# Three moves of single instructions in an RWKV time-mixing kernel: two products, five small copies, one scaling

## The chip, the core and the metric

The kernel runs on one core of a Trainium2 chip. The metric is the device time of one execution in microseconds. Before the change the median of 12 runs is 202.87 us, the lowest 202.19, the highest 204.02.

Five engines take part, each working through its own instructions in the order in which they were written: TensorE (PE, matmuls and transposes), VectorE (DVE), ScalarE (ACT), GpSimd (POOL) and SyncE (SP, which here issues DMAs). An instruction that needs a result of another engine waits on a semaphore, and all that stands behind it on its engine waits with it.

## The reference, cut to what matters

```python
x_prev[:, 1:, :] = x[:, :-1, :]                     # the row before, zero for the first
xv = x * time_mix_v + x_prev * (1 - time_mix_v)
xr = x * time_mix_r + x_prev * (1 - time_mix_r)
v = xv @ value_weight
r = xr @ receptance_weight
out = (sigmoid(r) * v) @ output_weight
```

x is 16 x 2048 x 256, float32. The key product k is computed by the reference but not used in its output, and the kernel leaves it away.

## The kernel before, in words

The 16 batches of 2048 rows are cut into 64 units of 512 rows (`NU`), four to a batch. The data is held transposed, channels on the 128 partitions, in two halves of the 256 channels (`ko` 0 and 1), as bf16. A unit u goes through these steps:

- Its rows are transposed into a tile `xt`, by PE and a copy on ACT (L207, L223), or, for the last five batches, by a transposing DMA on SP (L188). A batch's `xt` has one slot more than the batch has row groups: slot 0 holds the last group shifted by one column, so that the "row before" is the slot before. For batches 2 to 10 DVE makes this shifted slot (L427). For batches 11 to 15, whose rows come by DMA, ACT makes it (L550), in the windows 41, 45, 49, 53 and 57.
- Its two mixes, R and V, are formed in a tile `mix`. The mix of a row is c times the row before, plus the row, and a factor goes into the weights. First come the **products** `mix = xt * c`: the half ko = 0 mostly on DVE (L257, `scale`), the half ko = 1 of many early V mixes, and of all mixes from unit 10 on, on POOL (L267, `scale_pool`); from unit 10 on a product is for two units together (128x1024). Of the late units' V mixes the half ko = 0 is made on ACT (L514, `scale_act`). Then comes the **add** `mix = mix + xt` on DVE (L279, `add`).
- PE multiplies mix R by the receptance weights into `psum_r` (four matmuls, L287), ACT takes the sigmoid into `s_sb` (L535). PE multiplies mix V by the value weights into `psum_v` (L287), DVE forms z = s * psum_v (L580).
- PE multiplies z by the output weights into `psum_o` (eight matmuls, L311), ACT copies that to `o_sb` (L345), SP stores it.

`psum_r`, `psum_v` and `psum_o` have one buffer each. So the value matmuls of a unit wait until z of the unit before has been read out of `psum_v`, the receptance matmuls until the sigmoid before has read `psum_r`, and the output matmuls until the copy before has read `psum_o`.

The order is written out by hand: one pass of the loop at L522, a **window** g, issues for all engines what is to be done while unit g is projected. In the text r8, v8, z8, s8 and o8 are the receptance matmuls, value matmuls, z, sigmoid and output (matmuls, or the copy of them) of unit 8; "8R" and "8V" are its mixes. In a window PE does r_g, transposes for later units, v_g and o_(g-1); from unit 39 on (`LATE_O`) r_g, o_(g-2), v_g and no more transposes. DVE does the products due in this window, adds, z_g, and then the adds that are `held` until behind z. POOL does the products of `pooled[g]`, each made to wait for the last add in front of z_g (`scale_pool(p, last)`, L588). ACT does s_g, the copies of transposed rows, the copy of an output, and its products.

Lists built at L482 to L509 say which product and add is due in which window. In window 6 (`AHEAD`) DVE has, in front of z6: three products of unit 7 (7R both halves, 7V one half), two products of unit 8 (8R both halves, 128x512 each), the adds of 7R and 7V. The add of 8R is held behind z6. Mix V of the units 40 and 41 has its product for ko = 0 on ACT in window 38, since `FREE` is 38 and the test at L554 is `g >= FREE`. In the windows 41, 45, 49, 53 and 57 ACT does the sigmoid, then the shifted slot (L550), then the output's copy (L345). The product of POOL in these windows (mix R of units 44, 48, 52, 56, 60, the first of their batches) reads slot 0 of the new `xt`, so it needs this shifted slot as well as the last add.

Of the kernel before, what the change touches and what calls it, by code (L numbers as in the profile page):

```python
# [15 lines left out]
def kernel(  # L16
# [25 lines left out]
    nc = tc.nc  # L42

    B, S, D = x.shape
    P = 128
    KO = D // P
    J = S // P
    UJ = 4
    TU = UJ * P
    UB = J // UJ  # L50
# [4 lines left out]
    H = UJ // 2  # L55
    BYDMA = 5 * UB
    CROSS = NU - BYDMA - LOOK
    FREE = CROSS
    LATE_O = CROSS
    WAITING = {33: 38, 35: 39, 37: 43, 39: 43, 45: 51, 47: 51}  # L60
    START_T = [1, 3, 5, 6, 7, 9, 11, 12]
    AHEAD = 6
# [21 lines left out]
    xt = {}  # L84
# [14 lines left out]
    def unit_rows(t, b, e, n=1):  # L99

        return t[b, e * TU : (e + n) * TU, :].rearrange("(e p j) d -> p e j d", p=P, j=UJ)
# [21 lines left out]
    for m, tm in enumerate([time_mix_r, time_mix_v]):  # L123
        nc.scalar.dma_start(
            out=tm_rows[m * KO : (m + 1) * KO, :], in_=tm.rearrange("(ko p) -> ko p", p=P)
        )
    for h in (1, 0):
        nc.sync.dma_start(
            out=x_unit[:, 0, h * H : (h + 1) * H], in_=unit_rows(x, 0, 0)[:, 0, h * H : (h + 1) * H, :]
        )  # L130
    nc.sync.dma_start(
        out=w_f32[:, 0], in_=receptance_weight.rearrange("(ko p) n -> p ko n", p=P)
# [110 lines left out]
    def slots(piece, off=0):  # L243

        b, _, lo, hi = piece
        j = lo // P + (lo // TU if b < BYUNIT else 0) + off
        return slice(j, j + (hi - lo) // P)

    def mixed(piece):
        b, m, lo, hi = piece  # L250
        j = lo // P % (2 * UJ)
        return mix[(b * S + lo) // (2 * TU)][:, m, j : j + (hi - lo) // P]

    def scale(piece, kos=(0, 1)):
        b, m, _, _ = piece
        for ko in kos:
            nc.vector.tensor_scalar(  # L257
                out=mixed(piece)[:, :, ko],
                in0=xt[b][:, slots(piece), ko],
                scalar1=c_sb[:, m, ko : ko + 1],  # L260
                scalar2=None,
                op0=ALU.mult,
            )
# [13 lines left out]
    def add(piece):  # L277
        b = piece[0]
        return nc.vector.tensor_tensor(  # L279
            out=mixed(piece), in0=mixed(piece), in1=xt[b][:, slots(piece, 1)], op=ALU.add  # L280
        )
# [27 lines left out]
    def out_matmuls(ps, z, jj, slot):  # L309
        for ko in range(KO):  # L310
            nc.tensor.matmul(  # L311
                out=ps[:, slot, :],
                lhsT=z[:, ko, jj * P : (jj + 1) * P],
                rhs=wo_bf[:, ko, :],
                start=(ko == 0),
                stop=(ko == KO - 1),
            )

    def store(queue, b, lo, hi, after=None):
        dst = out[b].rearrange("(p j) d -> p j d", p=P)  # L320
        op = queue.dma_start(out=dst[:, lo:hi, :], in_=o_sb[b][:, lo:hi, :])
        if after is not None:
            tc.add_manual_dep(op.ins, after.ins.name, SYNC, reason="in turn with the last load")

    def out_part(pool, name, z, b, e, jj, n, copy, queue):
        ps = pool.tile([P, n, D], FP32, name=name)
        for k in range(n):
            out_matmuls(ps, z, jj + k, k)
        lo = e * UJ + jj
        copy(out=o_sb[b][:, lo : lo + n, :], in_=ps)  # L330
        store(queue, b, lo, lo + n)

    def output(g, z):
        b, e = divmod(g, UB)
        if e == 0:
            o_sb[b] = opool.tile([P, J, D], FP32, name="o_sb")
        j0 = e * UJ
        if g >= NU - 4:
            for h in range(2):
                out_part(ps_t_pool, "ps_t", z, b, e, h * H, H, nc.scalar.copy, nc.sync)  # L340
            return
        ps = ps_o_pool.tile([P, UJ, D], FP32, name="psum_o")
        for jj in range(UJ):
            out_matmuls(ps, z, jj, jj)
        nc.scalar.copy(out=o_sb[b][:, j0 : j0 + UJ, :], in_=ps)  # L345
        if b < BYUNIT:
            if e % 2 == 1:
                nc.sync.dma_start(
                    out=unit_rows(out, b, e - 1, 2),
                    in_=o_sb[b][:, j0 - UJ : j0 + UJ, :].rearrange("p (e j) d -> p e j d", j=UJ),  # L350
                )
        elif g >= NU - 8:
            store(nc.sync, b, j0, j0 + UJ)
        elif e % 2 == 1:
            pair = (b, j0 - UJ, j0 + UJ)
            if g in WAITING:
                kept.setdefault(WAITING[g], []).append(pair)
            else:
                store(nc.sync, *pair)
# [45 lines left out]
    def pieces(g):  # L405

        b, e = divmod(g, UB)
        tile_for(g // 2)
        return [(b, m, e * TU, (e + 1) * TU) for m in range(2)]
# [43 lines left out]
    for ko in range(KO):  # L453
        nc.vector.tensor_scalar(
            out=w_prev[:, ko, :],
# [6 lines left out]
        out=w_bf[:, 0, 0, :], in0=w_f32[:, 0, 0, :], scalar1=tms[:, 0, 0:1], scalar2=None, op0=ALU.mult  # L462
    )
    nc.scalar.activation(
        out=w_bf[:, 0, 1, :], in_=w_f32[:, 0, 1, :], func=ACT.Copy, scale=tms[:, 0, 1:2]
# [3 lines left out]
    for ko in range(KO):  # L469
        nc.vector.tensor_scalar(  # L470
            out=w_bf[:, 1, ko, :],
# [39 lines left out]
    def scale_act(piece, kos):  # L511
        b, m, _, _ = piece
        for ko in kos:
            nc.scalar.activation(  # L514
                out=mixed(piece)[:, :, ko],
                in_=xt[b][:, slots(piece), ko],
                func=ACT.Copy,
                scale=c_sb[:, m, ko : ko + 1],
            )

    z_prev2 = z_prev = None
    for g in range(NU - 1):  # L522
        ps_r = ps_r_pool.tile([P, KO, TU], FP32, name="psum_r")
        if g == 0:
            project_unmixed(ps_r, 0)
            advance(1)
            project_unmixed(ps_r, 1)
            for ko in range(KO):
                wrap_slots(pieces(1)[0], ko)
                scale(pieces(1)[0], (ko,))  # L530
            last = add(pieces(1)[0])
        else:
            project(ps_r, g, 0)
        s_sb = zpool.tile([P, KO, TU], BF16, name="s_sb")
        nc.scalar.activation(out=s_sb, in_=ps_r, func=ACT.Sigmoid)  # L535
        advance(START_T[g] if g < len(START_T) else g + LOOK - (g == CROSS - 1))
        for b in range(B - 5, B):
            if g == max(UB * (b - 2) - 1, CROSS + (b > B - 5)):
                new_xt(b)
                if b == B - 5:  # L540
                    for pair in kept.pop(g):
                        store(nc.sync, *pair, after=half_load)
                    by_dma(b, J - UJ, J, last_load)
                    by_dma(b, 0, J - UJ, last_load)
                else:
                    by_dma(b, 0, J)
                for pair in kept.pop(g, []):
                    store(nc.sync, *pair)
            if g == UB * (b - 1) + 1:
                nc.scalar.copy(out=xt[b][:, 0, :, 1:P], in_=xt[b][:, J, :, 0 : P - 1])  # L550
        if LATE_O < g < NU - 2:
            output(g - 2, z_prev2)
        for p in products.get(g + 1, []):
            if g >= FREE and p[0][1] == 1:  # L554
                scale_act(p[0], (0,))
        for p in [q for q, _ in products[g]] + pooled[g]:
            last_unit_of = p[3] // TU - 1
            need = last_unit_of if p[0] < BYUNIT else min(last_unit_of + 1, UB - 1)
            assert UB * p[0] + need < tnext, (g, p, tnext)
            if g > AHEAD or p not in pooled[g]:  # L560
                wrap_slots(p)
        if g == 1:
            scale_act(pieces(2)[1], (1,))
        for p, kos in products[g]:
            if not (g - 1 >= FREE and p[1] == 1):
                scale(p, kos)
        for p in sums[g]:
            last = add(p)
        for p in pooled[g]:
            if p[0] >= BYUNIT:  # L570
                wrap_slots(p)
        ps_v = ps_v_pool.tile([P, KO, TU], FP32, name="psum_v")
        project(ps_v, g, 1)
        if g == 0:
            scale_act(pieces(1)[1], (0,))
            advance(2)
        z_sb = zpool.tile([P, KO, TU], BF16, name="z_sb")
        n = TU // 2 if g == NU - 2 else TU
        for c in range(0, TU, n):
            nc.vector.tensor_tensor(  # L580
                out=z_sb[:, :, c : c + n],
                in0=s_sb[:, :, c : c + n],
                in1=ps_v[:, :, c : c + n],
                op=ALU.mult,
            )
        for p in pooled[g]:
            wrap_slots(p, after=last)
            scale_pool(p, last)  # L588
        for p in held[g]:
            add(p)  # L590
        if z_prev is not None and not LATE_O <= g < NU - 3:
            output(g - 1, z_prev)
        if g == 1:
            advance(4)
        z_prev2, z_prev = z_prev, z_sb
# [31 lines left out]
```

## Time and profile before

| what | value |
|---|---|
| median of 12 runs | 202.87 us (202.19 to 204.02) |
| the profiled execution: time / span from first to last instruction | 203.0 us / 200.9 us |
| granted TensorE clock | 0.996 |
| PE busy | 195.0 us, 97% of the span |
| DVE busy | 186.0 us, 93% |
| ACT busy | 180.2 us, 90% |
| POOL busy | 83.8 us, 42% |
| DMA | 57.26 MB, 338 GB/s of HBM traffic over the span |

How to read the timeline that the prediction shows: each line is an instruction (or several of a kind in a row, "x2"), with its start in us from the start of the span, its duration in us, the engine, the line of the kernel, the operation, what it writes and reads with the shapes, and in brackets how long its engine had been idle before it and what ended that. The recorded intervals of neighbouring instructions overlap by about 0.08 us on DVE and 0.1 us on ACT: an engine's pace is read from start to start and not from the durations.

### The profile page before, as it was taken

Reading aid. Unit: us, or ns where it says so; the run is one execution under the profiler, and the core shown is the slowest. Engines: PE = TensorE matmul, PEld = TensorE weight load, DVE = VectorE, ACT = ScalarE, POOL = GpSimd, SP = SyncE. Lnnn points to the kernel's source line nnn. Section 1 sums busy time; section 2 is a strip of 40 time slices with the busy share of each in tenths; the row PEclk is TensorE's granted clock in tenths of the full one; section 3 lists DMA queues with packets and bytes.
Section 4 is the critical chain, followed back from the end, with each engine's and each line's share of the span. In section 5 each row is a group of like instructions: output and inputs, shape, how many; then the busy total and the mean of one; then the engine's idle time right before and its main releaser. Section 6 shows DMA issues by size and latency. Waiting matters only on the chain.

```text
span 200.9 us, 3891 instructions
## 1 busy us (share of the span) xinstructions
PE 195.0 (97%) x1422; PEld 125.3 (62%) x1422; DVE 186.0 (93%) x296; ACT 180.2 (90%) x202; POOL 83.8 (42%) x115
## 2 busy tenths in 40 slices
PE   8799999999999999999999999999999999999993
PEld 6466675666666666666666666655656565555671
DVE  0899999999999999999999999999999999999982
ACT  3499999999999999999999999899999999999982
POOL 1746582434443534425434354343444444444200
PEclk9999999999999999999999999999999999999998
DMA  5899999999999999999999999999999999999575
GB/s 156 284 193 217 219 282 272 279 281 273 290 312 290 284 284 285 282 285 279 287 297 343 292 418 268 279 199 244 274 293 426 277 213 297 414 421 369 219 308 215
DMA packets 32298, 57.26 MB, mean 285 GB/s; under 512 B 21780, under 2 KB 23064, under 8 KB 28312
## 3 DMA queue, kind: packets, MB, share of 16 engines
q1 hardware_dynamic: 28208, 40.77, 59.8%
q0 software_dynamic: 3920, 16.12, 39.8%
q8 instruction: 11, 0.18, 0.4%
q10 hardware_dynamic: 152, 0.13, 0.2%
q14 instruction: 7, 0.06, 0.1%
HBM read 34.34 MB, written 33.55 MB: 338 GB/s over the span
## 4 chain that ended last, share of the span: by engine, by line
PE 81%; ACT 5%; DVE 5%; DMA 3%; issue 3%; SPq 1%; POOL 0%; DVEq 0%
PE psum_v L287 24%; PE psum_o L311 24%; PE psum_r L287 23%; PE ps_t L207 7%; DMA o_sb<-in_x_dram 3%; DVE mix L279 2%; ACT s_sb L535 2%; DVE z_sb L580 2%; PE ps_t L311 1%; DVE mix L257 1%; ACT mix L514 1%; ACT xt_first L223 1%; ACT xt L223 1%; ACT xt_first L216 0%; ACT o_sb L345 0%
## 5 line engine op out<-in xcount | busy, mean ns | idle before, releaser
L267 POOL TENSOR_SCALAR mix<-xt,c_sb 128x1024 bf16<-128x1024 bf16 (+1 forms) x55 | 61.0, 1109 | 92.6 <-DVE mix L279 80.6
L580 DVE TENSOR_TENSOR z_sb<-s_sb,psum_v 128x1024 bf16<-128x1024 bf16 (+1 forms) x64 | 76.7, 1200 | 3.6 <-PE psum_v L287 1.5
L279 DVE TENSOR_TENSOR mix<-mix,xt 128x1024 bf16<-128x1024 bf16 x112 | 77.0, 696 | 1.6
L287 PEld LDWEIGHTS <-w_bf 128*128 128x128 bf16 x516 | 48.7, 98 | 38.6 <-issue 0.7
L535 ACT ACTIVATE s_sb<-psum_r 128x1024 bf16<-128x1024 f32 x63 | 65.0, 1031 | 3.5 <-PE psum_r L287 2.7
L345 ACT COPY o_sb<-psum_o 128x1024 f32<-128x1024 f32 x60 | 61.1, 1019 | 7.1 <-PE psum_o L311 7.1
L287 PE MATMUL psum_v<-mix,w_bf 128*128 128x512 bf16 (+1 forms) x256 | 65.3, 377 | 0.3 <-DVE z_sb L580 0.2
L287 PE MATMUL psum_r<-mix,w_bf 128*128 128x512 bf16 (+1 forms) x252 | 64.2, 377 | 0.1
L311 PE MATMUL psum_o<-wo_bf,z_sb 128*128 128x256 bf16 x486 | 63.2, 272 | 0.0
L311 PEld LDWEIGHTS <-z_sb 128*128 128x128 bf16 x512 | 49.8, 98 | 20.5 <-issue 1.4
L223 ACT COPY xt<-ps_t 128x1024 bf16<-128x1024 bf16 x36 | 36.6, 1030 | 0.0
L207 PEld LDWEIGHTS <-x_bf 128*128 128x128 bf16 x328 | 21.5, 98 | 8.8
L207 PE MATMUL ps_t<-ident,x_bf 128*128 128x128 bf16 x328 | 24.5, 219 | 0.0
L257 DVE TENSOR_SCALAR mix<-xt,c_sb 128x1024 bf16<-128x1024 bf16 (+1 forms) x49 | 22.1, 458 | 0.0
L514 ACT ACTIVATE mix<-xt,c_sb 128x1024 bf16<-128x1024 bf16 x12 | 13.9, 1157 | 0.0
L279 DVE TENSOR_TENSOR mix<-mix,xt_first 128x1024 bf16<-128x1024 bf16 x15 | 10.6, 709 | 0.1
L114 POOL DMA_DIRECT2D x_bf<-in_x_dram x13 | 8.6, 658 | 0.0
L257 DVE TENSOR_SCALAR mix<-xt_first,c_sb 128x512 bf16<-128x512 bf16 x22 | 6.6, 350 | 0.2
L223 ACT COPY xt_first<-ps_t 128x1024 bf16<-128x1024 bf16 x5 | 5.2, 1035 | 0.0
L267 POOL TENSOR_SCALAR mix<-xt_first,c_sb 128x512 bf16<-128x512 bf16 x6 | 4.1, 686 | 1.2 <-DVE mix L279 0.6
L153 PE MATMUL ps_t<-zeros 128*128 128x128 bf16 x33 | 3.4, 284 | 1.0 <-DVE zeros L90 1.0
L427 POOL COPY xt_first<-xt_first 128x254 bf16<-128x254 bf16 x5 | 2.0, 393 | 5.5 <-DVE mix L279 5.4
(66 smaller groups left out, 50.6 us busy)
## 6 DMA issues: line engine op xcount, KB each, us to landing
out_dram<-o_sb SPq DMA_DIRECT2D x28, 1024.0 KB, 13.6
x_bf<-in_x_dram POOLq DMA_DIRECT2D x13, 1024.0 KB, 23.4
out_dram<-o_sb SPq DMA_DIRECT2D x4, 512.0 KB, 2.8
out_dram<-o_sb SPq DMA_DIRECT2D x6, 256.0 KB, 2.5
x_bf<-in_x_dram POOLq DMA_DIRECT2D x5, 256.0 KB, 7.0
o_sb<-in_x_dram SPq DMA_DIRECT2D x2, 512.0 KB, 5.8
x_bf<-in_x_dram POOLq DMA_DIRECT2D x2, 512.0 KB, 10.6
o_sb<-in_x_dram SPq DMA_DIRECT2D x2, 256.0 KB, 2.9
```

The source lines that it names most:

```text
L114: return nc.gpsimd.dma_start(out=x_bf[b], in_=rows(b), max_dma_last_dim=run)
L207: nc.tensor.transpose(out=ps[:, jj], in_=src[:, jj, ko * P : (ko + 1) * P], identity=idn)
L223: nc.scalar.copy(out=xt[b][:, j0 : j0 + UJ], in_=ps)
L257: nc.vector.tensor_scalar(out=mixed(piece)[:, :, ko], in0=xt[b][:, slots(piece), ko], scalar1=c_sb[:, m, ko : ko + 1], scalar2=None, op0=A ...
L267: op = nc.gpsimd.tensor_scalar(out=mixed(piece)[:, :, 1], in0=xt[b][:, slots(piece), 1], scalar1=c_sb[:, m, 1:2], scalar2=1.0, op0=ALU.mul ...
L279: return nc.vector.tensor_tensor(out=mixed(piece), in0=mixed(piece), in1=xt[b][:, slots(piece, 1)], op=ALU.add)
L287: nc.tensor.matmul(out=ps[:, mo, :], lhsT=w_bf[:, m, ko, mo * P : (mo + 1) * P], rhs=mixed((b, m, e * TU + lo, e * TU + hi))[:, :, ko], st ...
L311: nc.tensor.matmul(out=ps[:, slot, :], lhsT=z[:, ko, jj * P : (jj + 1) * P], rhs=wo_bf[:, ko, :], start=(ko == 0), stop=(ko == KO - 1),)
L345: nc.scalar.copy(out=o_sb[b][:, j0 : j0 + UJ, :], in_=ps)
L514: nc.scalar.activation(out=mixed(piece)[:, :, ko], in_=xt[b][:, slots(piece), ko], func=ACT.Copy, scale=c_sb[:, m, ko : ko + 1],)
L535: nc.scalar.activation(out=s_sb, in_=ps_r, func=ACT.Sigmoid)
L580: nc.vector.tensor_tensor(out=z_sb[:, :, c : c + n], in0=s_sb[:, :, c : c + n], in1=ps_v[:, :, c : c + n], op=ALU.mult,)
```

## The change

Three things are moved.

- In window 6 the two products of 8R on DVE are issued behind z6, just in front of the held add of 8R.
- In the windows 41, 45, 49, 53 and 57 the copy of the shifted slot on ACT is issued behind the copy of the output instead of in front of it.
- `FREE` is 39 instead of 38: the product of mix V of units 40 and 41 for ko = 0 goes from ACT in window 38 to DVE in window 39, in front of the add of 40V.

```diff
-    FREE = CROSS
+    FREE = CROSS + 1
...
-            if g == UB * (b - 1) + 1:
-                nc.scalar.copy(out=xt[b][:, 0, :, 1:P], in_=xt[b][:, J, :, 0 : P - 1])
         if LATE_O < g < NU - 2:
             output(g - 2, z_prev2)
+        if g % UB == 1 and B - 5 <= g // UB + 1 < B:
+            b = g // UB + 1
+            nc.scalar.copy(out=xt[b][:, 0, :, 1:P], in_=xt[b][:, J, :, 0 : P - 1])
         for p in products.get(g + 1, []):
             if g >= FREE and p[0][1] == 1:
                 scale_act(p[0], (0,))
...
+        behind_z = [pieces(AHEAD + 2)[0]] if g == AHEAD else []
         for p, kos in products[g]:
+            if p in behind_z:
+                continue
             if not (g - 1 >= FREE and p[1] == 1):
                 scale(p, kos)
...
         for p in held[g]:
+            if p in behind_z:
+                scale(p)
             add(p)
```

Nothing else differs: the orders on PE, SP and POOL are the same; one product of POOL (42R, in window 39) now names a wait on ACT that others implied before. ACT has one instruction fewer, DVE one more.

## The prediction

> **What bounds the kernel now.** I read the busy line and the clock first, then the chain of waits, then the timelines where that chain leaves PE.
>
> ```profile
> PE 195.0 (97%) x1422; PEld 125.3 (62%) x1422; DVE 186.0 (93%) x296; ACT 180.2 (90%) x202; POOL 83.8 (42%) x115
> ...
> PEclk9999999999999999999999999999999999999998
> ```
>
> PE is busy 97% at a granted clock of 0.996, so an edit can only win where PE stands still, and loses as soon as it makes PE stand still. The chain lies on PE from 33.8 us to 123.8 us and from 132 us almost to the end. The changed places are three: v7 at 33.81 us, which comes behind 0.24 us of idle time put down to z6 (the transposes before it would let it start at about 33.40, so 0.41 are lost); the turn to the late order around 124 to 132 us; and five output blocks, whose pieces in the chain last 0.98, 1.01, 1.01, 1.01 and 1.01 us where the others have 0.87. That is 0.11 + 4 x 0.14 = 0.67 us.
>
> DVE around the first place (timeline of DVE, and of PE and POOL):
>
> ```profile
> 30.82 0.61 DVE L257 TENSOR_SCALAR mix<-xt,c_sb 128x512 bf16<-128x512 bf16 x2
> 31.34 1.28 DVE L279 TENSOR_TENSOR mix<-mix,xt_first 128x1024 bf16<-128x1024 bf16 x2
> 32.55 1.21 DVE L580 TENSOR_TENSOR z_sb<-s_sb,psum_v 128x1024 bf16<-128x1024 bf16 x1
> 33.68 0.68 DVE L279 TENSOR_TENSOR mix<-mix,xt 128x1024 bf16<-128x1024 bf16 x1
> ...
> 40.91 0.48 DVE L257 TENSOR_SCALAR mix<-xt,c_sb 128x1024 bf16<-128x1024 bf16 x1
> 41.49 0.69 DVE L279 TENSOR_TENSOR mix<-mix,xt 128x1024 bf16<-128x1024 bf16 x1
> 42.10 1.22 DVE L580 TENSOR_TENSOR z_sb<-s_sb,psum_v 128x1024 bf16<-128x1024 bf16 x1
> 43.23 0.78 DVE L279 TENSOR_TENSOR mix<-mix,xt 128x1024 bf16<-128x1024 bf16 x1
> ```
> ```profile
> 32.79 0.69 POOL L267 TENSOR_SCALAR mix<-xt,c_sb 128x512 bf16<-128x512 bf16 x1 [3.36 <-ACT xt L223]
> ```
>
> No line of DVE from 30 to 43 us has idle time in brackets: each starts where the one before lets it. PE's waits on DVE follow a rule that can be read off: v(g+1) starts 1.26 us after z(g) (32.55 to 33.81), and z(g) 1.13 us after v(g) where it waits for it (136.37 to 137.50). By this rule v9 could start at 39.02 + 1.26 = 40.28 and starts at 40.35; v10 could start at 42.10 + 1.26 = 43.36 and starts at 43.39. So DVE is 0.03 us from being the bound.
>
> The late place, around the second of the five copies (timelines of ACT, PE, DVE, POOL):
>
> ```profile
> 146.46 1.02 ACT L535 ACTIVATE s_sb<-psum_r 128x1024 bf16<-128x1024 f32 x1
> 147.36 0.41 ACT L550 COPY xt<-xt 128x254 bf16<-128x254 bf16 x1
> 147.66 1.03 ACT L345 COPY o_sb<-psum_o 128x1024 f32<-128x1024 f32 x1
> ```
> ```profile
> 148.74 1.03 PE L311 MATMUL psum_o<-wo_bf,z_sb 128*128 128x256 bf16 x8
> ```
> ```profile
> 148.00 1.22 DVE L580 TENSOR_TENSOR z_sb<-s_sb,psum_v 128x1024 bf16<-128x1024 bf16 x1
> 149.14 0.74 DVE L279 TENSOR_TENSOR mix<-mix,xt 128x1024 bf16<-128x1024 bf16 x1
> 149.80 0.47 DVE L257 TENSOR_SCALAR mix<-xt,c_sb 128x1024 bf16<-128x1024 bf16 x1
> 150.20 0.68 DVE L279 TENSOR_TENSOR mix<-mix,xt 128x1024 bf16<-128x1024 bf16 x1
> 150.80 1.21 DVE L580 TENSOR_TENSOR z_sb<-s_sb,psum_v 128x1024 bf16<-128x1024 bf16 x1
> ```
> ```profile
> 148.22 1.12 POOL L267 TENSOR_SCALAR mix<-xt,c_sb 128x1024 bf16<-128x1024 bf16 x1 [1.39 <-DVE mix L279]
> ```
>
> The shifted slot takes 0.30 us of ACT ahead of the output's copy, and o44 starts at 148.74 instead of 148.60. POOL's product runs beside z45, and its tail touches the add.
>
> **How an add behaves beside POOL.** Over the whole trace, a DVE add that starts while POOL's product is still running steps on to the next instruction later, by how long they overlap: overlap 0.16 us, step 0.62 or 0.61 (0.60 undisturbed); 0.20, step 0.66 (149.14 to 149.80); 0.24, step 0.70 (54.92 to 55.62); 0.26, step 0.72 (49.00 to 49.72). Beyond about 0.145 us each further 0.01 of overlap costs 0.01: while POOL runs the add gets nowhere. POOL's product keeps 1.12 us throughout, and z is undisturbed. The other way round POOL gives way: its copy at 27.44 us, issued with the add at 27.45, takes 0.73 us where its like takes 0.20. No row overlaps by more than 0.26 us, and the trace alone does not show whether the hold lasts for the whole of a long overlap. The Trainium skill, "SBUF — State Buffer", section "Who interferes with whom", says that it does: an add with both inputs in SBUF shares a read port with a GpSimd instruction that reads SBUF, and the one that starts first keeps it to its end. That speaks against this change: by that page's rule the sum at the end is the forecast's +2.1 us, and if the rule did not reach so far it would be the first rival's -0.7. My own ground is the rows: I carry their slope of one on, as nothing in them levels off.
>
> **Part 2, the five copies (the large term).** The output's copy moves to 147.36 and o44 has no stall: a gain of 0.14 in a window. But the shifted slot now starts at 147.36 + 0.905 (step of an output's copy) = 148.27 and ends at 148.67. POOL's product reads that slot, so it starts not at 148.22 but at 148.67 + 0.09 (POOL's start at 32.79 behind ACT's copies that end at 32.70) = 148.76, and ends at 149.88. The add wants to start at 149.14: overlap 0.74, hold 0.74 - 0.145 = 0.60, in place of 0.06. z46 comes at 148.00 + 1.14 + 0.60 + 0.60 + 0.40 + 0.60 = 151.34, and v47 at 151.34 + 1.26 = 152.60, where before it was 152.21. So instead of winning 0.14 the window loses 0.39. It does not come back: z47 waits for v47 again, ACT's distance to PE is as before (its chain sigmoid, output, product of 0.92 + 0.90 + 1.05 = 2.87 us is longer than PE's 2.60 a unit, which is why the sigmoid of these windows is late), and POOL meets the next add in the same way. Four windows (45, 49, 53, 57): +1.56. Bounds for each: -0.14 with no hold, +0.49 if POOL wakes 0.1 later, as 148.22 stands 0.25 behind its add where 153.40 stands 0.17 behind. The new wait queues nothing else: the next product of POOL is due at 150.97. ACT is free again at 148.57, before s46 at 148.79.
>
> **Part 3, unit 40's product.** ACT loses 1.05 us in window 38, s39 starts at about 130.2 instead of 130.91, and the 0.24 us before r40 (132.00) go. DVE gets a product of 0.40 us, and the add of 40V directly behind it must wait for it: such a pair steps 0.58 (40.91 to 41.49), a pair of different mixes 0.40 (43.93 to 44.33). Before, the two adds behind z38 ended just as z39 could start (132.03 = v39 at 130.90 + 1.13), so nothing covers it: z39 at 129.64 + 1.13 + 0.61 + 0.58 + 0.60 = 132.56, v40 at 133.82 (133.77 before). POOL's 42R is released by that add and meets the next one by 0.24: +0.10, so z40 at 132.56 + 2.84 = 135.40, v41 at 136.66 (136.37 before: +0.29). In window 41, the first with a copy, ACT is now not late: POOL starts at about 138.06, ends at 139.18, the add behind z41 (137.79) starts at 138.93: overlap 0.25, hold 0.11. z42 at 140.64, v43 at 141.90 against 141.67 before, in which a stall of 0.11 is gone. Parts 3 and the first copy together: **+0.23**. Without the wait of the pair and without holds it is -0.13 (v43 at 141.54); with ACT late in window 41 as in the others up to +0.6.
>
> **Part 1, 8R behind z6.** The adds start at 30.82, z6 at 32.03, v7 at 33.40: 0.41 won there. Then the products start at 33.16, beside POOL's product until 33.48. Nothing shows a product so met; between nothing and an add's hold (0.32 - 0.145 = 0.175) I take the hold, the nearest row. The add of 8R has to wait for its own product, which costs 0.18 as above. It ends its step at 33.16 + 0.175 + 0.52 + 0.18 + 0.60 = 34.64 instead of 34.28. DVE has no idle time until z9, so z7, z8, z9 come 0.36 to 0.37 later: v8 at 37.30 (unchanged), v9 at 40.65 (40.35), v10 at 43.73 (43.39). From z10 on DVE has room, and +0.34 stays. With neither cost DVE's sum is what it was, and v10 wins only the 0.03 it has: bounds -0.03 and +0.34, taken **+0.34**.
>
> **The sum.** +0.34 + 0.23 + 1.56 = +2.13 us. The profiled execution had 203.0 us (span 200.9, 2.1 around it), which gives 205.1; the median of the runs is 0.13 lower, so **205.0**. Bounds: -0.03 - 0.13 - 0.56 = -0.7 and 0.34 + 0.6 + 4 x 0.49 = +2.9.
>
> **The rivals.**
> - *The hold does not last.* Place: the add behind z45, z49, z53, z57. The waits that the change aims at go, and nothing replaces them: -0.7, 202.1 us. The point where this turns: v47 stays at or below 152.21 if the hold is at most 0.21, an overlap of 0.36, so if POOL ended by 149.50. For it: no row over 0.26 of overlap. Against it: a slope of one with no sign of levelling.
> - *Half.* Parts 1 and 3 cost little (the pair's wait overlaps something), or POOL starts earlier than I reckon: four windows at 0.2 to 0.3 and some 0.2 beside, +0.5 to +1.4, 203.4 to 204.3.
> - *DVE goes first.* If POOL wakes only at 149.14, the add runs first, POOL waits as its copy at 27.44 did, and the following product or add then waits for 1.1 us: four times some +0.9, 206.8. Against it: 0.38 us of distance.
> - That the moves don't happen is excluded by the order of the instructions.
>
> **How the numbers follow.** Forecast 205.0 (204.4 to 205.9): 0.67. Half: 0.14. The hold does not last, or costs just what is won (202.1 to 203.2): 0.16. DVE first: 0.03. About 0.3%, 0.61 us, can be told from no change. Slower by more: 0.67 + 0.03 + most of half = 0.82; within: 0.09; faster: 0.09. The range 202.7 to 205.9 takes in half and a part of the third case.
>
> **What would show it.** Right: POOL's L267 waits for ACT's shifted slot five times; the adds behind z45, z49, z53, z57 are recorded with about 1.28 us instead of 0.74; PE is idle about 0.5 us before v47, v51, v55, v59, put down to z; o44 has no stall; v7 starts at 33.40 and v10 at 43.7. Wrong: adds of 0.7 to 0.8 us beside a POOL product of 1.12, or a product of POOL that is stretched instead; v10 at 43.4 or before.

## The result, and the profile after

The changed kernel takes **204.97 us** (median of 12 runs, 204.35 to 205.51) against 202.83 us (49 runs of the kernel before): the ratio is 1.0096, 95% interval 1.0080 to 1.0112. It is 2.1 us slower. The span of the profiled execution is 203.2 us, before it was 200.9.

The chain that ended last by engine, on the page of the kernel before:

```profile
PE 81%; ACT 5%; DVE 5%; DMA 3%; issue 3%; SPq 1%; POOL 0%; DVEq 0%
```

The page of the changed kernel, its busy line and the same chain:

```profile
PE 196.5 (97%) x1422; PEld 125.6 (62%) x1422; DVE 188.9 (93%) x297; ACT 178.7 (88%) x201; POOL 83.9 (41%) x115
...
PE 62%; DVE 16%; ACT 10%; issue 7%; DMA 3%; SPq 1%; DVEq 0%
```

PE's share of the chain falls from 81% to 62%, that of DVE rises from 5% to 16%: PE now waits for DVE again and again in the last third. The same place as in the prediction, window 45, in the changed kernel (timelines of ACT, PE, DVE and POOL; an edit shifts the line numbers, so that L553 here is the shifted slot's L550 and L584 is the L580 of z):

```profile
147.11 1.02 ACT L535 ACTIVATE s_sb<-psum_r 128x1024 bf16<-128x1024 f32 x1
148.01 1.02 ACT L345 COPY o_sb<-psum_o 128x1024 f32<-128x1024 f32 x1
148.90 0.43 ACT L553 COPY xt<-xt 128x254 bf16<-128x254 bf16 x1
```
```profile
148.38 1.03 PE L287 MATMUL psum_r<-mix,w_bf 128*128 128x512 bf16 x4
149.24 1.04 PE L311 MATMUL psum_o<-wo_bf,z_sb 128*128 128x256 bf16 x8
150.12 1.03 PE L287 MATMUL psum_v<-mix,w_bf 128*128 128x512 bf16 x4
151.14 1.04 PE L287 MATMUL psum_r<-mix,w_bf 128*128 128x512 bf16 x4
152.02 1.04 PE L311 MATMUL psum_o<-wo_bf,z_sb 128*128 128x256 bf16 x8
153.27 1.02 PE L287 MATMUL psum_v<-mix,w_bf 128*128 128x512 bf16 x4 [0.21 <-DVE z_sb L584]
```
```profile
148.65 1.22 DVE L584 TENSOR_TENSOR z_sb<-s_sb,psum_v 128x1024 bf16<-128x1024 bf16 x1
149.79 1.29 DVE L279 TENSOR_TENSOR mix<-mix,xt 128x1024 bf16<-128x1024 bf16 x1
151.01 0.47 DVE L257 TENSOR_SCALAR mix<-xt,c_sb 128x1024 bf16<-128x1024 bf16 x1
151.40 0.68 DVE L279 TENSOR_TENSOR mix<-mix,xt 128x1024 bf16<-128x1024 bf16 x1
152.01 1.21 DVE L584 TENSOR_TENSOR z_sb<-s_sb,psum_v 128x1024 bf16<-128x1024 bf16 x1
```
```profile
149.43 1.12 POOL L267 TENSOR_SCALAR mix<-xt,c_sb 128x1024 bf16<-128x1024 bf16 x1 [1.92 <-PE psum_r L287]
```

o44 has lost its stall: it starts 0.86 us behind r46 (148.38), where before it was 1.01 (148.74 behind r46 at 147.73). But the shifted slot ends at 149.33, POOL's product starts 0.10 later and runs to 150.55, and the add that wants to run from 149.79 is recorded with 1.29 us instead of 0.74. Its step is 1.22, so it was held 0.62. Before, it was held 0.06, and z46 comes later behind z45 by the difference: 3.36 us instead of 2.80. PE loses in two places: r47 starts 1.02 behind v46 instead of 0.86, 0.06 behind the end of the held add, and v47 starts 0.38 later than its pace behind o45 (0.87) would let it, 1.26 behind z46. Less the 0.14 won at o44, that is the window's 0.40 to 0.41. Note the releaser that the profile names for POOL: r46, which happens to end at 149.41. POOL's product does not need r46 (before, it started while r46 still ran); the time of the start, 0.10 behind the shifted slot, is the better witness.

Window 6 in the changed kernel (DVE, then POOL):

```profile
32.33 1.21 DVE L584 TENSOR_TENSOR z_sb<-s_sb,psum_v 128x1024 bf16<-128x1024 bf16 x1
33.46 0.60 DVE L257 TENSOR_SCALAR mix<-xt,c_sb 128x512 bf16<-128x512 bf16 x2
34.09 0.69 DVE L279 TENSOR_TENSOR mix<-mix,xt 128x1024 bf16<-128x1024 bf16 x1
34.70 0.87 DVE L257 TENSOR_SCALAR mix<-xt,c_sb 128x512 bf16<-128x512 bf16 x3
```
```profile
32.57 0.69 POOL L267 TENSOR_SCALAR mix<-xt,c_sb 128x512 bf16<-128x512 bf16 x1 [2.84 <-DVE mix L279]
```

The two products step 0.63 to their add, where they stepped 0.52 before: the pair's wait costs 0.11 to 0.12. POOL's product is through at 33.26, before the products start. All of this execution is 0.30 us later already at v5 (27.13 against 26.83), ahead of anything that the change touches.

**A measure for the parts.** Between executions the first 26 us vary: v5 starts between 26.18 and 28.78 us in the profiles of this study (in the latest of them PE waits 1.28 us for a load of x, until 6.15 us). Behind v5 they agree to 0.01 us as far as the code is the same. So I read the start of the value matmuls v from PE's timeline, count from v5, and take the difference from the kernel before:

| kernel | v7 | v10 | v41 | v45 | v49 | v53 | v57 | v61 |
|---|---|---|---|---|---|---|---|---|
| changed kernel | -0.44 | +0.10 | +0.39 | +0.35 | +0.75 | +1.16 | +1.57 | +1.97 |
| only part 1 | -0.44 | +0.11 | +0.11 | +0.11 | +0.11 | +0.11 | +0.11 | +0.11 |
| only part 2 | 0 | 0 | 0 | +0.41 | +0.82 | +1.23 | +1.64 | +2.04 |
| only part 3 | +0.01 | +0.01 | +0.30 | +0.26 | +0.27 | +0.27 | +0.27 | +0.27 |
| parts 1 and 3 | -0.44 | +0.10 | +0.39 | +0.35 | +0.35 | +0.35 | +0.35 | +0.35 |
| part 1 apart | -0.44 | -0.02 | -0.03 | -0.02 | -0.02 | -0.02 | -0.02 | -0.02 |
| POOL late | +0.01 | +0.01 | +0.01 | +0.48 | +0.89 | +1.30 | +1.71 | +2.18 |
| POOL behind the add | 0 | +0.01 | 0 | +0.59 | +1.15 | +1.71 | +2.27 | +2.83 |
| slot 0 on ACT | +0.01 | +0.01 | 0 | -0.02 | -0.09 | -0.15 | -0.22 | -0.28 |
| early copies | 0 | 0 | 0 | +0.01 | -0.13 | -0.24 | -0.12 | -0.26 |
| combined | -0.44 | -0.03 | -0.04 | -0.07 | -0.21 | -0.35 | -0.39 | -0.53 |

### The profile page after: what moved, and what is told of

Same layout as the page of the kernel before. It is cut to its first block, busy times and chain, and to the rows that moved or that the text cites. A ratio compares the mean times of both kernels' runs of the same rounds, so it can differ in the third digit from the quotient of the medians.

```text
span 203.2 us, 3891 instructions
## 1 busy us (share of the span) xinstructions
PE 196.5 (97%) x1422; PEld 125.6 (62%) x1422; DVE 188.9 (93%) x297; ACT 178.7 (88%) x201; POOL 83.9 (41%) x115
## 4 chain that ended last, share of the span: by engine, by line
PE 62%; DVE 16%; ACT 10%; issue 7%; DMA 3%; SPq 1%; DVEq 0%
PE psum_v L287 19%; PE psum_r L287 17%; PE psum_o L311 15%; PE ps_t L207 8%; DVE z_sb L584 8%; DVE mix L279 7%; ACT s_sb L535 4%; DMA o_sb<-in_x_dram 3%; ACT o_sb L345 3%; ACT xt L223 3%; PE ps_t L311 1%; DVE mix L257 1%; PE ps_t L287 0%; PE psum_r L301 0%; SPq L128 0%
## 5 line engine op out<-in xcount | busy, mean ns | idle before, releaser
L279 DVE TENSOR_TENSOR mix<-mix,xt 128x1024 bf16<-128x1024 bf16 x112 | 79.6, 719 | 1.7
L584 DVE TENSOR_TENSOR z_sb<-s_sb,psum_v 128x1024 bf16<-128x1024 bf16 (+1 forms) x64 | 76.6, 1199 | 2.6 <-PE psum_v L287 1.4
L345 ACT COPY o_sb<-psum_o 128x1024 f32<-128x1024 f32 x60 | 61.1, 1018 | 7.4 <-PE psum_o L311 7.4
L514 ACT ACTIVATE mix<-xt,c_sb 128x1024 bf16<-128x1024 bf16 x11 | 12.8, 1161 | 0.0
```

The costliest lines, as they stand in the source:

```text
L279: return nc.vector.tensor_tensor(out=mixed(piece), in0=mixed(piece), in1=xt[b][:, slots(piece, 1)], op=ALU.add)
L514: nc.scalar.activation(out=mixed(piece)[:, :, ko], in_=xt[b][:, slots(piece), ko], func=ACT.Copy, scale=c_sb[:, m, ko : ko + 1],)
L584: nc.vector.tensor_tensor(out=z_sb[:, :, c : c + n], in0=s_sb[:, :, c : c + n], in1=ps_v[:, :, c : c + n], op=ALU.mult,)
```

## The experiments

The theory: the five copies cost because they hold back POOL's product, which then holds DVE's add; parts 1 and 3 cost because DVE has no room where they put work. The main rival: the new order on ACT itself, or the product gone from ACT to DVE, costs the time.

**Each part alone.** The edits are the three parts of the diff, one at a time.

> Part 1 alone (8R's products behind z6). The prediction's term: +0.34 us (0.175 for a hold of the first product beside POOL's product of 8V, 0.18 for the wait of the add of 8R for its own product). Theory after the trace of the changed kernel: POOL's product of 8V waits for the add of 7V, which also comes 0.52 us earlier, so it is through before DVE's product starts and there is no hold; only the wait of the pair is left, read there as 0.11: v10 about +0.10 us behind the kernel before, whole kernel +0.1. Rival, as the stall at v7 suggests: the 0.41 us won at v7 stay, -0.4.

202.91 us against 203.18, ratio 0.9992 (0.9959 to 1.0025): not told from no change. The profile tells it: +0.11 at v10, and it stays. The 0.44 us are won at v7 and are gone at v9. Theory, not the rival.

> Part 2 alone (the five shifted slots behind the output's copy). Theory (POOL's product starts later, meets the add behind z and holds it for 0.6 us): ACT is late in all five windows here, so each of the windows 41, 45, 49, 53, 57 loses 0.4 us, together +2.0. Rival (the loss of the changed kernel comes from the other parts, or from ACT's product gone to DVE): the five stalls of 0.11 to 0.14 us before the output matmuls go, -0.67.

204.90 against 203.18, ratio 1.0098 (1.0063 to 1.0132): this part alone gives a slowdown as large as the whole change's (1.0096). By the table, +0.41 in each of five windows, +2.04 in all, as the theory had it.

> Part 3 alone (the product of 40V for ko = 0 back on DVE). Theory: DVE has no room in window 39; the product of 0.40 and the wait of the add of 40V for it push z39 to z40, v41 comes 0.29 later, but the stall of 0.11 before the output matmuls of window 41 goes, as ACT is no longer late there: +0.2 in all. Rival: the stall of 0.24 before r40 goes and nothing takes its place, -0.2 to -0.3.

203.26 against 203.18, ratio 0.9997 (0.9968 to 1.0025). In the table +0.30 at v41, +0.20 at v42, then +0.27: the theory's +0.2, and 0.07 more.

**Parts 1 and 3 together** (the changed kernel without part 2).

> The changed kernel with the five copies put back in front. Theory (parts 1 and 3 cost 0.11 and 0.27 and do not meet each other): v63 comes 0.38 us behind the kernel before, counted from v5. Against the 1.98 of the changed kernel the copies then cost 1.60 there, four windows at 0.40, while alone they cost 2.05: the first window is free once unit 40's product has left ACT. Rival (the parts interact elsewhere): anything but 0.35 to 0.41.

+0.35 (a single run, 203.0 us). So in the changed kernel the copies cost 1.97 - 0.35 = 1.62, four windows at 0.40 or 0.41, and the first is free. The lines of the changed kernel in window 41 (ACT's shifted slot; POOL's product; the add) say why: without the product of unit 40, ACT is early enough in window 41, POOL is through 0.27 us after the add's start, and the hold is only 0.13 (without part 2 the add of this window has the same 0.81).

```profile
137.97 0.42 ACT L553 COPY xt<-xt 128x254 bf16<-128x254 bf16 x1
```
```profile
138.48 1.12 POOL L267 TENSOR_SCALAR mix<-xt,c_sb 128x1024 bf16<-128x1024 bf16 x1 [1.39 <-ACT xt L553]
```
```profile
139.33 0.81 DVE L279 TENSOR_TENSOR mix<-mix,xt 128x1024 bf16<-128x1024 bf16 x1
```

**The wait of the pair (part 1 apart).** Part 1, with the add of 8R in window 7 behind that window's products:

```diff
             if p in behind_z:
                 scale(p)
+                continue
             add(p)
...
+        if g == AHEAD + 1:
+            add(pieces(g + 1)[0])
         for p in sums[g]:
             last = add(p)
```

> Part 1 alone, but the add of 8R goes behind the three products of window 7, so that it no longer stands right behind its own product. Theory (all that part 1 costs is the wait of that pair, 0.12 us on DVE): v10 comes at the time of the kernel before or 0.03 earlier, counted from v5, instead of 0.11 later. Rival (the costs lie elsewhere, in POOL's product or in the order of the products): 0.1 later as with part 1 alone.

v10 at -0.02 (a single run, 202.42 us). DVE's five products and two adds, now without a gap between them:

```profile
32.67 1.40 DVE L257 TENSOR_SCALAR mix<-xt,c_sb 128x512 bf16<-128x512 bf16 x5
33.98 1.29 DVE L279 TENSOR_TENSOR mix<-mix,xt 128x1024 bf16<-128x1024 bf16 x2
```

The five products step 1.31, or 0.26 each, and no wait follows. All that part 1 cost was the add right behind its own product; without it, it is worth the 0.02 to 0.03 that DVE leaves.

**POOL's product late, nothing moved on ACT.** The kernel before, with the start of POOL's product tied to the output's copy:

```diff
-            scale_pool(p, last)
+            scale_pool(p, o_copy[0] if g % UB == 1 and g > LATE_O else last)
```

(`o_copy[0]` is the last copy at L345.)

> The kernel before with nothing moved on ACT or DVE, but POOL's product in the windows 41, 45, 49, 53, 57 waits for the output's copy instead of the last add, and so starts about 0.5 us later, as it does in the changed kernel. Theory (POOL's product meets the add and holds it): overlap 0.7 to 0.76, hold 0.56 to 0.6, each window about +0.39, in all +1.95 us; the stalls of 0.14 before the output matmuls stay. Rival (the order on ACT is what costs): no change.

205.55 against 203.03, ratio 1.0116 (1.0075 to 1.0157). DVE and POOL in window 45 of this kernel, where ACT's shifted slot is still in front of the output's copy:

```profile
148.97 1.30 DVE L281 TENSOR_TENSOR mix<-mix,xt 128x1024 bf16<-128x1024 bf16 x1
150.19 0.47 DVE L258 TENSOR_SCALAR mix<-xt,c_sb 128x1024 bf16<-128x1024 bf16 x1
```
```profile
148.62 1.12 POOL L268 TENSOR_SCALAR mix<-xt,c_sb 128x1024 bf16<-128x1024 bf16 x1 [1.91 <-ACT o_sb L347]
```

The overlap is 0.77 and the step 1.22: held 0.62, which is 0.77 - 0.145. With ACT's order as before, the late product alone makes the loss, 0.41 in each of the three middle windows and 0.47 in the first and the last, where the overlap is longer (0.79 and 0.83, steps 1.25 and 1.29). The rival of ACT's order falls.

**DVE first.** POOL's product behind the held add (the loop over `held[g]` ahead of the one over `pooled[g]` in these windows, with `last = add(p)`).

> The kernel before, but in the windows 41, 45, 49, 53, 57 POOL's product waits for the held add behind z, so that DVE's next product is already running when POOL becomes ready. This is the case 'DVE goes first'. Theory (whoever starts first keeps the other out to its end): POOL waits for DVE's product, then either gets in before the next add and holds it for about 1 us (each window +0.7 to +0.9, in all +3.5 to +4.5), or is kept out by that add as well and runs beside z (then within 0.3 us of the kernel before). Rival (they share, each slowed): POOL's product and DVE's add both stretched by some tenths.

206.46 against 203.03, ratio 1.0164 (1.0118 to 1.0209); +0.56 to +0.59 a window. In window 45 POOL starts at 152.62, in DVE's product:

```profile
152.28 0.48 DVE L257 TENSOR_SCALAR mix<-xt,c_sb 128x1024 bf16<-128x1024 bf16 x1
152.68 0.69 DVE L279 TENSOR_TENSOR mix<-mix,xt 128x1024 bf16<-128x1024 bf16 x1
153.28 1.21 DVE L580 TENSOR_TENSOR z_sb<-s_sb,psum_v 128x1024 bf16<-128x1024 bf16 x1
154.41 2.09 DVE L279 TENSOR_TENSOR mix<-mix,xt 128x1024 bf16<-128x1024 bf16 x2
```
```profile
152.62 1.65 POOL L267 TENSOR_SCALAR mix<-xt,c_sb 128x1024 bf16<-128x1024 bf16 x1 [3.18 <-DVE mix L279]
```

DVE's product and add keep their 0.48 and 0.69; it is POOL's product that is stretched, from 1.12 to 1.65. The hold of 1 us that I expected in this window, and that the third rival of the prediction rested on, does not come in the order tried here. The price comes one window later: POOL's next product is behind this one, runs to about 155.4 and holds the two adds behind z46, which take 2.09 where they took 1.30: an overlap of 0.95, a hold of 0.79. Nearest to the theory's second branch in the first window, and neither in its sum.

**The copy in its new place, without POOL waiting for it.** Part 2, with POOL's product of these windows on slots 1 to 7 only, and on ACT behind the shifted slot:

```diff
+            nc.scalar.activation(
+                out=mixed(p)[:, 0:1, 1], in_=xt[b][:, 0:1, 1], func=ACT.Copy, scale=c_sb[:, 0, 1:2]
+            )
...
-            out=mixed(piece)[:, :, 1],
-            in0=xt[b][:, slots(piece), 1],
+            out=mixed(piece)[:, n0:, 1],
+            in0=xt[b][:, slots(piece), 1][:, n0:],
```

> Part 2 alone, but POOL's product of the five windows leaves slot 0 out (7 slots of 8), and ACT makes slot 0's product for ko = 1 itself behind the shifted slot (128x128). So the copy stands where the change puts it, and POOL does not wait for it. The result is the reference's. Theory (what costs is only that POOL's product meets the add): POOL starts right behind the last add again, no add is held, the stalls before the output matmuls are gone: five times -0.14 or -0.11, about -0.6 us. Rival (the order on ACT itself costs, by a later sigmoid or a later copy of the next output): +1.5 to +2 as in the changed kernel, or more, since ACT does one instruction more.

202.66 against 203.18, ratio 0.9984 (0.9953 to 1.0015). In window 45 (DVE, POOL):

```profile
149.00 0.68 DVE L280 TENSOR_TENSOR mix<-mix,xt 128x1024 bf16<-128x1024 bf16 x1
```
```profile
147.98 1.01 POOL L268 TENSOR_SCALAR mix<-xt,c_sb 128x896 bf16<-128x896 bf16 x1 [1.30 <-PE psum_v L288]
```

POOL starts 1.02 us ahead of the add, which runs undisturbed in 0.68, though ACT has the changed kernel's order and one instruction more. Each stall of 0.14 is won; 0.07 of it is lost again between v47 and v48, where r48 and o46 wait 0.04 and 0.03 for a sigmoid and a copy that ACT's extra product (0.40 us) has made late. Half of what the theory expected in size.

**The copy two windows sooner.** Batches 12 to 15 in the windows 43, 47, 51, 55, behind the output's copy.

```diff
-            if g == UB * (b - 1) + 1:
+            if b == B - 5 and g == UB * (b - 1) + 1:
...
+        if g % UB == UB - 1 and B - 5 < g // UB + 2 < B and g > LATE_O + 1:
+            b = g // UB + 2
+            nc.scalar.copy(out=xt[b][:, 0, :, 1:P], in_=xt[b][:, J, :, 0 : P - 1])
```

> The kernel before, but the shifted slots of batches 12 to 15 are copied two windows sooner (43, 47, 51, 55), behind the output's copy, where ACT has 0.45 us of idle time before the next sigmoid; batch 11 stays. Theory (the copy costs only by its place in front of an output's copy, or by holding back POOL's product): POOL's product starts right behind the last add, no add is held, four stalls of 0.14 are gone, -0.56 us. Rival 1: DVE, which has 0.07 us of room per pair of windows, becomes the bound: -0.2 or less. Rival 2: the rows of the transposing DMA are not there two windows sooner, ACT waits for them and all behind it: slower by 1 us or more.

203.02 against 203.03, ratio 0.9991 (0.9964 to 1.0018). The windows 45, 49 and 57 win 0.13 to 0.14 each. In window 51 the second rival comes true, in a small way (ACT):

```profile
163.92 1.02 ACT L345 COPY o_sb<-psum_o 128x1024 f32<-128x1024 f32 x1
165.51 0.40 ACT L555 COPY xt<-xt 128x254 bf16<-128x254 bf16 x1 [0.56 <-DMA xt<-x_bf]
```

Batch 14's rows arrive 0.56 us after ACT is ready for them, ACT's sigmoids and copies of the windows 52 and 53 are late by it, and from v51 to v54 0.15 us are lost, the gain of window 53 already counted. In all -0.26 at v61 is left of the -0.56 that the theory expected.

**Combined.** Part 1 apart; batches 12, 13 and 15 sooner, batches 11 and 14 with slot 0 on ACT; unit 40's product stays on ACT.

> A version built from the runs so far: 8R's products behind z6 with the add of 8R apart from them; the shifted slots of batches 12, 13 and 15 copied two windows sooner (batch 14's rows were not there yet); batches 11 and 14 behind the output's copy with slot 0's product on ACT; unit 40's product stays on ACT. Counted from v5, the pieces measured so far give -0.02 (part 1 apart), three times -0.13 (early copies), about -0.1 and -0.07 (slot 0 on ACT): -0.55 to -0.6 us at v63. Rival: DVE's room of 0.07 us per pair of windows is used up by the first of them, -0.3 or less. The times of the runs scatter by more than this; the profile decides.

**202.03 us** against 202.62, ratio 0.9963 (0.9937 to 0.9990), and -0.53 at v61, close to the -0.55 to -0.6 that its measured pieces add up to: faster than the kernel before.

## Why the prediction was right, and where it was not

The predicted 205.0 us and +2.1 were met by 204.97 and a difference of 2.14. By its steps:

- **Part 2, four windows.** Predicted +0.39 each and 1.56 together. Measured +0.40, +0.41, +0.41, +0.40, or 1.62. The slope of one, read from overlaps of 0.16 to 0.26, holds at 0.76 (149.43 to 150.55 against an add at 149.79: 0.62) and, with POOL late, from 0.77 to 0.83 (0.62 to 0.69). So carrying the rows' slope of one on was the right choice, and the first rival, a hold that does not last, is refuted. The other signs named for a window: the add is recorded with 1.29 (1.28 forecast); PE's loss of about 0.5 is 0.54, but only 0.38 of it stands before v47, and 0.16 before r47, which the prediction left out. The rule of the Trainium skill, "SBUF — State Buffer", section "Who interferes with whom", that the first to start keeps a port that two-input adds share with GpSimd for its whole instruction, agrees where POOL was first: DVE's add was held by 0.62. Where DVE was first, POOL gave way and its product was stretched by 0.53; but it was kept out by a product and then by the add behind that, and what happens with two such DVE instructions in a row the section does not say. The runs show who waits and how long, not which port it is.
- **Part 3 and the first copy.** Predicted +0.23, measured 0.35 - 0.10 = +0.25 at v45. v41 was to be 0.29 later for part 3 and is (+0.39 - 0.10). ACT is early in window 41 as forecast, and the hold there was 0.13 for 0.11.
- **Part 1.** Predicted +0.34, measured +0.10 to +0.11: the term of the sum that was mis-sized. The step that failed is "the products start at 33.16, beside POOL's product until 33.48". I took POOL's start at 32.79 as fixed, because the profile puts its wait down to a copy on ACT. But `scale_pool` ties that product to the last add in front of z6, and the change brings this add 0.52 us forward. The row itself allowed the other reading: that add ended at 31.34 + 1.28 = 32.62, and POOL's usual 0.17 behind an add gives 32.79. So there was no overlap and no hold. The other half of the term, the pair's wait, was 0.12 for 0.18; the row it came from was of a product of twice the length, and whether that makes the difference was not tried. Part 1 apart shows that this wait was all of the cost. So v10 came at 43.49 on the clock of the kernel before, between the 43.7 named as the sign of right and the 43.4 named as the sign of wrong. That a product of DVE is held by POOL was not tried.
- **The sum.** 2.13 was predicted; the parts measure 0.10 + 0.25 + 1.62 = 1.97. Most of the predicted time is from the term that was right. That the medians differ by 2.14, as forecast to 0.01, is in part luck: the term of part 1 was 0.24 too large, the other two were 0.08 too small, and the interval of the ratio reaches from 1.6 to 2.3 us. The span's difference of 2.3 holds 0.30 from before v5, which no edit touches.
- **The aims of the change.** Its three stalls were real and each went: 0.44 at v7, 0.24 before r40, 0.11 to 0.14 at each output. What took their place is late on DVE: z7 to z9, z39 and z40, and the add behind z45 and its like.

## What to carry to other kernels

Where two engines take turns at a resource, an instruction that is moved also moves what it releases: before moving the source of a wait, look at what will run beside the released instruction, and for how long. Where an engine is as full as DVE is here (93% busy), a stall that is taken away by reordering can return a window or two later, as the 0.44 at v7 did by v9, unless the sum of that engine's work, its waits between dependent neighbours included, has room. A releaser that a profile names is the last event before a start and not always its cause: hold it against the waits in the code before you take a start time as fixed.

## What the runs showed of the hardware that I had not expected

When DVE was first, POOL's product was kept out behind DVE's product and its add in turn (1.65 us instead of 1.12), though the record has POOL starting before that add (152.62 against 152.68); the loss then came from POOL's own queue, a window later. And behind the first 26 us the kernels agree to 0.01 us in the start of every block of value matmuls for as long as their code is the same, while whole runs scatter by about 2 us: at v5 the profiles already differ by up to 2.6 us. A single profile read block by block resolved effects here that 12 timed runs could not.
